# A small early write to the output, and the last store pieces issued from another queue

## The chip, the cores and the metric

The kernel runs on one core of a Trainium2 chip. The metric is the device time of one execution in microseconds (us). The time before is 471.92 us (median of 4 runs, 471.72 to 472.5; the prediction had only the first three, with a median of 471.87). The span in the profile is about 1.8 us shorter than the time, because it begins with the first recorded work. One core can show no difference between two dies, so the profiled runs with several timings are called fast by their closeness to each other; a run with a single timing has the state unknown, and of those only the trace is read here, never a time difference of a few tenths. Each trace is of one execution.

## The reference

```python
def setup_inputs():
    batch, seq, dim = (32, 512, 2048)
    return {'x': np.random.randn(batch, seq, dim).astype(np.float32)}

def reference(x):
    half_dim = x.shape[-1] // 2
    x1, x2 = (x[..., :half_dim].copy(), x[..., half_dim:].copy())
    silu_x1 = x1 * (1 / (1 + np.exp(-x1)))
    return (silu_x1 * x2).astype(np.float32)
```

So 134.2 MB are read, 67.1 MB are written, and each element gets one activation and one multiply.

## The kernel before

The profile names the engines ACT (ScalarE), DVE (VectorE), SP (SyncE, which only issues transfers here) and POOL. What SP issues and what ACT issues go through two DMA queues, and both queues are served by the same 16 DMA engines; a packet is what a DMA engine moves in one go, 64 KB of a load or 32 KB of a store here.

There are 16 tiles of 128 partitions by 8 rows. A load brings 8.4 MB and is issued from SP; a store takes 4.2 MB away and is issued from ACT. ScalarE and VectorE work on a tile in four pieces of two rows. Only the last tile is also stored in four pieces.

```python
K = 8; KC = 2
in_pool  = ctx.enter_context(tc.tile_pool(name="in_pool", bufs=2))
out_pool = ctx.enter_context(tc.tile_pool(name="out_pool", bufs=2))
xv = x_flat.rearrange("(n p k) d -> n p k d", p=P, k=K)
ov = out_flat.rearrange("(n p k) d -> n p k d", p=P, k=K)
# ... load(i): nc.sync.dma_start(out=xt, in_=xv[i])
load(0)
load(1)
for i in range(n_tiles):
    xt = loaded.pop(i)
    last = i == n_tiles - 1
    ot = out_pool.tile([P, K, half], dt, name="ot")
    for c in range(0, K, KC):
        ce = c + KC
        nc.scalar.activation(out=ot[:, c:ce, :], in_=xt[:, c:ce, :half], func=Silu)  # (name cut)
        nc.vector.tensor_mul(out=ot[:, c:ce, :], in0=ot[:, c:ce, :], in1=xt[:, c:ce, half:])
        if last:
            nc.scalar.dma_start(out=ov[i][:, c:ce, :], in_=ot[:, c:ce, :])
    if not last:
        nc.scalar.dma_start(out=ov[i], in_=ot)
    if i + 2 < n_tiles:
        load(i + 2)
```

Of the kernel before, what the change touches and what calls it, by code (L numbers as in the profile page):

```python
# [1 line left out]

# [4 lines left out]


@with_exitstack
def kernel(  # L10
    ctx: ExitStack,
    tc: tile.TileContext,
    x: bass.AP,
    out: bass.AP,
):





    nc = tc.nc
    P = nc.NUM_PARTITIONS

    x_flat = x.flatten_outer_dims()
    out_flat = out.flatten_outer_dims()
    num_rows, in_cols = x_flat.shape
    half = in_cols // 2
    dt = x_flat.dtype

    K = 8  # L30
    KC = 2
    n_tiles = num_rows // (P * K)
    assert n_tiles * P * K == num_rows

    in_pool = ctx.enter_context(tc.tile_pool(name="in_pool", bufs=2))
    out_pool = ctx.enter_context(tc.tile_pool(name="out_pool", bufs=2))

    xv = x_flat.rearrange("(n p k) d -> n p k d", p=P, k=K)
    ov = out_flat.rearrange("(n p k) d -> n p k d", p=P, k=K)

    loaded = {}

    def load(i):
        xt = in_pool.tile([P, K, in_cols], dt, name="xt")
        nc.sync.dma_start(out=xt, in_=xv[i])  # L45
        loaded[i] = xt
# [9 lines that stand above are left out]
            nc.scalar.activation(  # L56
                out=ot[:, c:ce, :],
                in_=xt[:, c:ce, :half],
                func=mybir.ActivationFunctionType.Silu,
            )  # L60
            nc.vector.tensor_mul(  # L61
                out=ot[:, c:ce, :],
                in0=ot[:, c:ce, :],
                in1=xt[:, c:ce, half:],
            )
            if last:
                nc.scalar.dma_start(out=ov[i][:, c:ce, :], in_=ot[:, c:ce, :])  # L67
        if not last:
            nc.scalar.dma_start(out=ov[i], in_=ot)
        if i + 2 < n_tiles:  # L70
            load(i + 2)


# [1 line left out]
_INS = ['x']  # L75
_OUTS = [((32, 512, 1024), 'float32')]


# [23 lines left out]
```

## Time and profile before

| What | Value |
|---|---|
| time | 471.92 us |
| span of the profiled run | 470.1 us |
| bytes moved by DMA | 201.35 MB, 428 GB/s over the span |
| VectorE, ScalarE busy | 30%, 25% |
| first store issued | 33.62 us |
| last load landed | 451.97 us |
| last store piece issued | 465.37 us |

From the page of the kernel before: the span, the busy time of two engines, the DMA row (one digit for each of 40 slices, 9 is 90% busy or more), and the issues with their size and the time from issue to landing.

```profile
span 470.1 us, 267 instructions
DVE 142.4 (30%) x64; ACT 118.3 (25%) x65; POOL 0.2 (0%) x4
DMA  8999999999999999999999999999999999999998
...
out_dram<-ot ACTq DMA_DIRECT2D x15, 4096.0 KB, 39.7
out_dram<-ot ACTq DMA_DIRECT2D x4, 1024.0 KB, 5.4
xt<-in_x_dram SPq DMA_DIRECT2D x16, 47.1
```

The DMA engines are the bound: they are busy in every slice, while no compute engine reaches a third. One period of the chain that ended last (start, length, what):

```profile
56.76 47.04 DMA xt<-in_x_dram
...
103.89 1.92 ACT ot L56
...
105.83 8.91 DVE ot L61 x4
...
114.75 47.19 DMA xt<-in_x_dram
```

From 56.76 to 114.75 us are 58.0 us for two tiles of 12.58 MB, so 434 GB/s. Only the two ends of the execution can give anything.

The timeline of the last tile (start, length, engine, line, operation, in brackets the idle time before it and who ended it), and below it the one entry of the waits list for ScalarE that belongs to the tail:

```profile
452.05 5.51 ACT L56 ACTIVATE ot<-xt 128x2048 f32<-128x2048 f32 x3 [21.65 <-DMA xt<-in_x_dram]
453.99 6.70 DVE L61 TENSOR_TENSOR ot<-ot,xt 128x2048 f32<-128x2048 f32 x3 [20.06 <-ACT ot L56]
456.32 4.74 ACTq L67 DMA_DIRECT2D out_dram<-ot  x3
461.11 1.91 ACT L56 ACTIVATE ot<-xt 128x2048 f32<-128x2048 f32 x1 [3.54 <-DVE ot L61]
463.05 2.29 DVE L61 TENSOR_TENSOR ot<-ot,xt 128x2048 f32<-128x2048 f32 x1 [2.36 <-ACT ot L56]
465.37 0.34 ACTq L67 DMA_DIRECT2D out_dram<-ot  x1
```

```profile
ACT ot L56 <- DVE ot L61: 3.5, 1, 3.5
```

The three issues on ACT wait for their multiplies, and the fourth activation stands behind them in ACT's program: it starts 3.54 us late, so the last piece is issued 13.4 us after the last load landed (465.37 - 451.97).

Three stretches of the windows view (window, length, busy time of DVE, ACT and POOL with counts, clock, share of the DMA engines, GB/s). This view books a packet whole at one instant, so a window in which no engine passes from one packet to the next shows 0 although the engines are at work.

```profile
37.00:39.40 2.40, 0.00 (x0) 0.00 (x0) 0.00 (x0) 1.00 0.00 0
458.00:460.00 2.00, 2.00 (x2) 0.00 (x0) 0.00 (x0) 1.00 0.97 410
465.00:466.50 1.50, 0.34 (x1) 0.00 (x0) 0.00 (x0) 1.00 0.37 153
```

An undisturbed 64 KB load packet takes 2.42 us and the engines are not all in phase. That no engine changes packets for 2.4 us after 37 us is unusual; the packet records say why. Here is one engine around the first store (queue, bytes, start, end):

```
load   65536   33.80   36.24
load   65536   36.24   39.55     <- 3.31 us instead of 2.42
store  32768   39.54   40.76
load   65536   40.75   43.17
```

All 16 engines have one such packet, and no later store has it. I call the surplus over the usual duration a *stretch*, and quote the sum over the engines divided by 16: 0.95 us here. The last window above is the idle time before the last piece.

### The profile page before, as it was taken

To read this page: it belongs to the slowest core of one execution; us is meant where nothing else is said; L and a number is where in the kernel's file an instruction comes from. 1 tells how busy PE (TensorE), PEld (TensorE's weight loads), DVE (VectorE), ACT (ScalarE), POOL (GpSimd) and SP (SyncE) were. 2 spreads that over 40 slices of the span, in tenths; PEclk is the share of its full clock that TensorE was granted. 3 is DMA by queue.
4 is the path that set the end of the run, shared out by engine and by line. 5 is a ranking of instruction groups with operands and counts; after the bars stand their busy time and mean duration, and the time that the engine had idled before them with its cause. 6 is when DMAs were issued, how large, how long until landed. Compare 5 with 4: busy or idle time off the path is not lost.

```text
span 470.1 us, 267 instructions
## 1 busy us (share of the span) xinstructions
DVE 142.4 (30%) x64; ACT 118.3 (25%) x65; POOL 0.2 (0%) x4
## 2 busy tenths in 40 slices
DVE  0070704207052070511606115070250702407033
ACT  1050506014060240602306032060320604106041
POOL 0000000000000000000000000000000000000000
DMA  8999999999999999999999999999999999999998
GB/s 357 446 446 401 401 485 435 418 401 443 449 446 401 441 457 396 446 474 390 468 404 438 457 441 407 427 420 449 446 410 432 480 401 418 440 474 424 399 424 337
DMA packets 5042, 201.35 MB, mean 428 GB/s; under 512 B 560, under 2 KB 560, under 8 KB 560
## 3 DMA queue, kind: packets, MB, share of 16 engines
q1 hardware_dynamic: 2304, 134.22, 66.2%
q10 hardware_dynamic: 2736, 67.11, 33.1%
q14 instruction: 2, 0.02, 0.0%
HBM read 134.22 MB, written 67.11 MB: 428 GB/s over the span
## 4 chain that ended last, share of the span: by engine, by line
DMA 80%; DVE 15%; ACT 4%; issue 0%; ACTq 0%; SPq 0%
DMA xt<-in_x_dram 80%; DVE ot L61 15%; ACT ot L56 4%; SPq L45 0%; ACTq L67 0%; ACTq L56 0%
## 5 line engine op out<-in xcount | busy, mean ns | idle before, releaser
L61 DVE TENSOR_TENSOR ot<-ot,xt 128x2048 f32<-128x2048 f32 x64 | 142.4, 2286 | 322.9 <-ACT ot L56 322.9
L56 ACT ACTIVATE ot<-xt 128x2048 f32<-128x2048 f32 x64 | 117.1, 1898 | 344.0 <-DMA xt<-in_x_dram 340.4
L56 ACT ACT_TABLE_LOAD x1 | 1.3, 1283 | 0.7 <-PEq L86 0.7
L86 POOL MEMSET const-bfloat16-1.0<- 128x1 bf16 x1 | 0.1, 101 | 0.0
L86 POOL MEMSET const-uint8-127<- 128x1 uint8 x1 | 0.1, 101 | 0.0
L86 POOL MEMSET const-float32-0.0<- 128x1 f32 x1 | 0.1, 98 | 0.2 <-issue 0.2
L86 POOL MEMSET const-float32-1.0<- 128x1 f32 x1 | 0.1, 98 | 0.0
## 6 DMA issues: line engine op xcount, KB each, us to landing
out_dram<-ot ACTq DMA_DIRECT2D x15, 4096.0 KB, 39.7
out_dram<-ot ACTq DMA_DIRECT2D x4, 1024.0 KB, 5.4
xt<-in_x_dram SPq DMA_DIRECT2D x16, 47.1
```

The lines of the kernel that those rows point to most:

```text
L56: nc.scalar.activation(out=ot[:, c:ce, :], in_=xt[:, c:ce, :half], func=mybir.ActivationFunctionType.Silu,)
L61: nc.vector.tensor_mul(out=ot[:, c:ce, :], in0=ot[:, c:ce, :], in1=xt[:, c:ce, half:],)
L86: nc = _bacc.Bacc("TRN2", target_bir_lowering=False, num_devices=1)
```

## The change

The intent: let each DMA engine do its first write to the output at the start, where nothing is lost, so that it does not cost 1 us at the first store; and let SP, which has nothing to do at the end, issue the last pieces, so that ScalarE's last activation is not held back.

```diff
+    first_pool = ctx.enter_context(tc.tile_pool(name="first_pool", bufs=1))
+    zt = first_pool.tile([16, 128], dt, name="zt")
+    nc.vector.memset(zt, 0.0)
+    nc.scalar.dma_start(out=ov[0][:16, 0, :128], in_=zt)
 
     loaded = {}
 # ... cut
             if last:
-                nc.scalar.dma_start(out=ov[i][:, c:ce, :], in_=ot[:, c:ce, :])
+                nc.sync.dma_start(out=ov[i][:, c:ce, :], in_=ot[:, c:ce, :])
```

The 16 rows of 512 bytes fall one on each DMA engine. The store of tile 0 overwrites them.

## The prediction

> **What bounds the kernel.** The DMA engines: the page's DMA row reads 9 in nearly every slice, 201.35 MB at 428 GB/s; VectorE is busy 30%, ScalarE 25%. The chain of waits repeats every 58.1 us for two tiles, so 25.17 MB / 58.1 us = 433 GB/s. The Trainium skill, "DMA: Bandwidth & Descriptors", section "Where 436 GB/s comes from", gives a ceiling of 435; this trace agrees, so the middle can't be shortened. By the packet records each engine moves 128 load packets of 64 KB (2.42 us), 120 store packets of 32 KB (1.21) and 32 of 8 KB (0.31): 465 us of the 470.1 us span. The other 5 us: 1.73 to the first packet, 0.7 by which the first load packet is longer, about 0.9 at the first store, 0.1 to 1.4 near the end, 1.3 after the last packet.
>
> **Part 1, the small write.** The first store is issued at 33.62 us. On all 16 engines one packet is stretched then: the load packet that begins at 36.2 to 36.9 us takes about 3.4 us instead of 2.42, so each engine loses 0.75 to 1.12 us (median about 0.97). No later store shows it. It delays all later loads and lies wholly on the critical path. The change lets each engine write 512 bytes at the start, where the first load packet is itself still waiting. It adds a VectorE memset (about 0.1 us, estimated from POOL's memsets) and an ACT issue (about 0.35 us), while both idle until 22.7 us. Store 0's wait on the small write is satisfied long before. If the stretch is a once-only cost of an engine's first write and overlaps the first load's start, up to 0.97 us is gained; if merely moved to the start, nothing; if it belongs to a queue that wakes from idle, or to the first mixing of loads and stores, it stays at 36 us. I expect 0.6 us on average.
>
> **Part 2, the last pieces from SP.** On ACT the issues of pieces 0 to 2 wait for VectorE and hold back the last activation (timeline: it starts at 461.11 us after 3.5 us of waiting for DVE). From SP, the activations run back to back, the last multiply ends near 453.99 + 4 x 2.23 = 462.9 instead of 465.34, and piece 3 is issued 2.4 us earlier. But the DMA engines have pieces 1 and 2 until 465.0 to 466.14 us; they idle only until piece 3 starts at 466.2 to 466.36: most over 1 us, the slowest 0.07 us. The slowest sets the end, so about 0.2 us is gained, up to 1 us if that engine (it lost 1.0 us near 314 us) isn't late this time. I expect 0.3 us.
>
> **Prediction.** 471.87 - 0.6 - 0.3 = 471.0 us, 8 in 10 between 470.1 and 472.0. Faster by over 2%: 0.01; within 2%: 0.98; slower: 0.01.
>
> **What would show it.** Right: no stretched packet or rate dip at 36 to 40 us; load 1 lands near 45.0 us instead of 45.87; the period stays 58.1 us; ScalarE's last four activations are contiguous; no engine idles between the last pieces. Wrong: the dip at 36 us remains (part 1 void), or the first load lands about 1 us later than 22.73 us (cost only moved), or a stretch appears at SP's first store (cost per queue).
>
> **What would make it wrong.** Mainly the stretch being tied to the queue's wake-up; else noise of some 0.4 us.

## The result

| | before | after |
|---|---|---|
| time, median | 471.92 us (4 runs) | 472.0 us (4 runs, 471.62 to 472.25) |
| span of the profiled run | 470.1 us | 470.5 us |
| stretch near 36 us, mean of 16 engines | 0.95 us | 1.07 us |
| stretch near 458 us | 0 | 0.61 us |
| idle of the engines in the tail | 0.92 us | 0.01 us |
| end of the last packet: median engine, last engine | 468.80, 468.88 us | 468.62, 469.14 us |

The ratio is 0.9999, with a 95% interval of 0.9982 to 1.0016: the same. (A ratio here is the mean time of one kernel's fast runs over that of the other's of the same rounds, so not quite the ratio of the medians quoted.) The rows three to six come from the packet records of the two profiled runs. Idle in the tail is the mean time in which an engine has no data packet, from the end of the last load packet to the first engine's end.

From the page of the kernel after:

```profile
span 470.5 us, 272 instructions
DVE 142.5 (30%) x65; ACT 118.2 (25%) x65; POOL 0.2 (0%) x4
...
out_dram<-ot SPq DMA_DIRECT2D x4, 1024.0 KB, 5.8
xt<-in_x_dram SPq DMA_DIRECT2D x16, 47.1
out_dram<-zt ACTq DMA_DIRECT2D x1, 8.0 KB, 9.7
```

The timeline of the last tile after:

```profile
452.50 7.31 ACT L64 ACTIVATE ot<-xt 128x2048 f32<-128x2048 f32 x4 [21.59 <-DMA xt<-in_x_dram]
454.44 8.90 DVE L69 TENSOR_TENSOR ot<-ot,xt 128x2048 f32<-128x2048 f32 x4 [20.00 <-ACT ot L64]
456.76 6.94 SPq L75 DMA_DIRECT2D out_dram<-ot  x4
```

The four activations are contiguous. The last multiply ends at 463.34 us, 10.9 us after the last load landed at 452.41 us, where it was 13.4 us before. This part did what it was meant to.

The same three windows after:

```profile
37.00:39.40 2.40, 0.00 (x0) 0.00 (x0) 0.00 (x0) 1.00 0.00 0
458.00:460.00 2.00, 2.00 (x2) 1.80 (x2) 0.00 (x0) 1.00 0.85 287
465.00:466.50 1.50, 0.00 (x0) 0.00 (x0) 0.00 (x0) 1.00 1.02 431
```

The window at 37 us is as it was: the early write removed nothing. The window at 465 us went from 153 to 431 GB/s: the idle time before the last piece is gone. But the window at 458 us fell from 410 to 287 GB/s: there is a new hole, where the first packet of SP's first piece takes up to 1.34 us instead of 0.31 (on 13 engines by more than 0.3 us). SP's first store also takes long to issue. These are the durations of the four issues from SP, shortest, median and longest, in ns:

```profile
L75 SPq DMA_DIRECT2D out_dram<-ot x4: 332/340/1057, 456.8 to 463.4; - x4
```

### The profile page after: what moved, and what is told of

Its sections match the earlier page's. It is cut to its first block, busy times and chain, and to the rows that moved or that the text cites. A ratio compares the mean times of both kernels' runs of the same rounds, so it can differ in the third digit from the quotient of the medians.

```text
span 470.5 us, 272 instructions
## 1 busy us (share of the span) xinstructions
DVE 142.5 (30%) x65; ACT 118.2 (25%) x65; POOL 0.2 (0%) x4
## 4 chain that ended last, share of the span: by engine, by line
DMA 80%; DVE 15%; ACT 3%; DVEq 0%; issue 0%; SPq 0%; ACTq 0%
DMA xt<-in_x_dram 80%; DVE ot L69 15%; ACT ot L64 3%; DVEq L105 0%; SPq L53 0%; ACTq L64 0%
```

## The experiments

Each run has one profile; those with 5 rounds also have times. The first questions are to which half of the change each finding belongs, and what the stretch at 36 us belongs to. Theory A: it is what a queue costs when it starts from empty beside a busy one. Theory B: it is a once-only cost of the first full-size store of a queue.

### The small write alone

The change without its second half (pieces again from `nc.scalar`).

> The small write alone, the last pieces issued from ACT as before. Theory A (a queue that wakes from idle beside a streaming queue stalls the DMA engines once, each time) and theory B (the first full-size store of a queue stalls it, once): the load packet stretched by about 1.0 us near 36 us stays, load 1 lands near 45.9 to 46.0 us, the tail is that of the kernel before (DMA engines idle about 1 us before the last piece), time within 0.3 us of before. My prediction's theory (first write of an engine, hidden at the start): stretch gone, load 1 lands near 45.0, time 0.6 to 1.0 us lower.

The time was 472.05 us against 471.98 (ratio 1.0005, 0.9993 to 1.0018). The stretch near 36 us was 0.82 us on average, on all 16 engines, and nothing was stretched near 458 us. So the small write does nothing for the first store, and the hole at 458 us is not its doing. Load 1 landed at 46.9 us rather than near 46.0, because one engine lost 1.34 us at 37 us and 0.67 us more at 42 us.

### The last pieces from SP alone

The change without the small write.

> The last pieces from SP alone, no small write. Theories A and B: the stretch at 36 us as before; near 458 us the first packet of SP's first store is longer by about 0.8 us on most engines, and the idle 1 us before the last piece is gone, so the time is within 0.4 us of before. If the small write were what costs in the tail, there would be no stretch at 458 us and the time would be 0.2 to 0.5 us lower.

The time was 471.92 us against 471.98 (1.0003, 0.9989 to 1.0016). The stretch at 458 us was 0.59 us, the idle time before the last piece 0.01 us. Both tail effects, the gain and the new loss, belong to the move to SP.

### The small write late, while the loads stream

```diff
-    nc.vector.memset(zt, 0.0)
-    nc.scalar.dma_start(out=ov[0][:16, 0, :128], in_=zt)
 # ... in the loop
+        if i == 0:
+            nc.vector.tensor_copy(out=zt, in_=xt[:16, 0, :128])
+            nc.scalar.dma_start(out=ov[0][:16, 0, :128], in_=zt)
```

> The small write is issued near 23 us instead of 1 us (it waits for a copy from tile 0), while load 1 streams alone. Theory A (wake from idle): a load packet near 25 to 28 us is stretched by about 1 us on each engine, and since the store queue is idle again by 33 us, another near 36 us. Theory B (first full-size store): nothing near 25 us, the stretch near 36 us as before.

The timeline line of the small write, and the window at 37 us:

```profile
22.82 0.38 ACTq L62 DMA_DIRECT2D out_dram<-zt  x1
```

```profile
37.00:39.40 2.40, 0.00 (x0) 0.00 (x0) 0.00 (x0) 1.00 0.00 0
```

No packet between 10 and 30 us was stretched, though the queue started from empty beside streaming loads; the stretch at 36 us stayed (0.91 us). Theory A, as a cost of any start, falls: and the stretch was not merely hidden in the start of the execution either. (A small write alone could not rule out that only large packets pay for a start. The two runs with an early packet of 32 KB, below, do: ACT's queue was empty again before the first regular store, and no packet at it was longer by more than 0.12 us.)

### One store in the middle from SP

```diff
-            nc.scalar.dma_start(out=ov[i], in_=ot)
+            eng = nc.sync if i == 7 else nc.scalar
+            eng.dma_start(out=ov[i], in_=ot)
```

with the last pieces from SP, without the small write.

> The store of tile 7 goes from SP, so that ACT's store queue runs empty before the store of tile 8 wakes it, and SP has issued a full-size store long before its tail pieces. Theory A: no stretch when SP issues store 7 (its queue is busy with loads), about 1 us per engine when ACT issues store 8 (near 295 us), and again about 0.8 us near 458 us. Theory B: a stretch at store 7 only, none at store 8, none at 458 us. A third, that SP's first store is merely slow to issue (1.06 us after the change, 0.34 for the others): 0.34 us issue and no stretch at 458 us here.

Store 7 was the first full-size store of SP's queue, and nothing was stretched at it. ACT's queue had run empty, and when store 8 (issued at 256.91 us, not near 295 us as I had written) woke it, the packets were 0.12 to 0.29 us longer, not 1 us. The first kills theory B in its form "per queue"; the second shows that a restart of the queue later costs far less. The stretch at 36 us belongs to the execution's first full-size store, then, not to each queue's.

In the tail SP's issues were no longer slow:

```profile
L67 SPq DMA_DIRECT2D out_dram<-ot x4: 332/338/344, 457.5 to 464.1; - x4
L70 SPq DMA_DIRECT2D out_dram<-ot x1: 348/348/348, 230.5 to 230.5; - x1
```

14 engines had no stretch there, but they did not win: the loads landed later (the last tile's work starts at 453.28 us, not at 452.05), the store queue was drained by 458.0 to 458.4 us, and most of those engines simply stood idle for 0.1 to 0.6 us. The two engines that were still busy when SP's piece came (until 458.62 and 458.86 us) were stretched by 0.8 and 0.9 us.

### All stores from SP

```diff
-            nc.scalar.dma_start(out=ov[i], in_=ot)
+            nc.sync.dma_start(out=ov[i], in_=ot)
```

and the last pieces from SP as well.

> Every store goes from SP, in the queue of the loads; ACT's queue is never used. If the stretch of 1 us at the first store belongs to the first full-size store of an execution, whatever its queue: a packet longer by about 1 us stands at the change from load 1 to store 0 (near 41 us). If it belongs to the second queue's start: no stretched packet after the first load's. In the tail SP's stores are warm, so issues of 0.34 us and no gap between pieces. Time: without the stretch 470.2 to 470.8 us, with it 471.0 to 471.6 us; if one queue cannot overlap loads and stores as well as two do, slower than before by several us.

The time was 475.69 us against 471.9 (1.0084, 1.007 to 1.0098): clear of the noise. The first two lines are windows of this run: one at its first store, one over the middle; the line in the second fence is the same middle window of the kernel before.

```profile
39.20:42.00 2.80, 0.00 (x0) 0.00 (x0) 0.00 (x0) 1.00 0.00 0
60.00:440.00 380.00, 115.66 (x52) 95.02 (x52) 0.00 (x0) 1.00 1.00 432
```

```profile
60.00:440.00 380.00, 115.67 (x52) 95.02 (x52) 0.00 (x0) 1.00 1.00 434
```

The stretch came at the change from load 1 to store 0, 1.20 us on average, in a queue that had been busy since the start. So it does not need a second queue. The loss comes on top: in one queue, the load packet before a store is on some engines 0.2 to 0.5 us longer, at nearly every tile (1.22 us per engine in the middle, 0.06 before), unevenly, so that the last engine ended at 471.48 us and the median one at 468.58. Whether this is the same effect in a weaker form is not shown; if it is, the stretch is once-only in two queues alone. Two queues are worth keeping for this kernel.

### What size must the early write have?

Three kernels with another early write from ACT, and the last pieces from ACT. First one packet of 32 KB on each engine (16 rows of 32 KB, from an output buffer):

```diff
+    zt = out_pool.tile([P, K, half], dt, name="ot")
+    nc.vector.memset(zt[:16], 0.0)
+    nc.scalar.dma_start(out=ov[0][:16], in_=zt[:16])
```

> The early write is one packet of 32 KB on each engine, the size of a store packet, instead of 512 bytes; it is issued some us after the start because its memset is longer. If the stretch belongs to the first full-size store packet: a stretched packet of about 1 us near 10 to 15 us and none at 36 us, so the time is about 1.2 us above before (the 512 KB written twice) or the same plus 1.2. If it belongs to many packets (a full store with 8 per engine) or to the first load-and-store mix of the kernel proper: stays near 36 us.

Then eight packets of 4 KB on each engine, the same bytes:

```diff
+    zt = first_pool.tile([128, 1024], dt, name="zt")
+    nc.vector.memset(zt, 0.0)
+    nc.scalar.dma_start(out=ov[0][:, 0, :], in_=zt)
```

> The early write is 8 descriptors of 4 KB on each engine (128 rows), issued near 2 us. Same question as with one packet of 32 KB, by count instead of packet size. If the count or the bytes matter: no stretch at 36 us (it is at the start or hidden there). If only the packet size matters: the stretch stays at 36 us, about 1.0 us.

Then eight packets of 512 bytes on each engine:

```diff
+    zt = first_pool.tile([128, 128], dt, name="zt")
+    nc.vector.memset(zt, 0.0)
+    nc.scalar.dma_start(out=ov[0][:, 0, :128], in_=zt)
```

> The early write is 8 descriptors of 512 bytes on each engine (128 rows by 128 columns): the count of a full store at the size of the small write, 64 KB in all. If the count matters: no stretch at 36 us and the time lower by 0.5 to 1 us. If bytes or packet size matter: the stretch of about 1.0 us stays at 36 us.

Windows at the first regular store: the first fence is the run with one packet of 32 KB, the second that with eight of 4 KB. That store is issued at 36.07 us in the first and at 34.77 us in the second, not at 33.62 us, so the windows lie later.

```profile
38.40:40.80 2.40, 0.00 (x0) 0.00 (x0) 0.00 (x0) 1.00 0.98 423
```

```profile
38.20:40.60 2.40, 0.00 (x0) 0.00 (x0) 0.00 (x0) 1.00 0.00 0
```

Only the one packet of 32 KB took the stretch away: no packet between 30 and 45 us was stretched. With eight packets of 4 KB it was 0.88 us, with eight of 512 bytes 1.09 us. Bytes and count are therefore not what matters, the size of a packet is. The 32 KB packet did not come free: 1.35 us of stretch per engine stood between 12 and 18 us, on the load packets and on the early packet itself. The early write was also extra traffic of 0.5 MB (1.2 us by the duration of a 32 KB packet), and both big writes had a span of 471.7 us, above the 470.1 of before.

### The same large packet from another buffer

The run before took its packet from an output buffer, the small writes from a buffer of their own. To part that from size, one packet of 32 KB on each engine was stored out of the first load's buffer:

```diff
+        if i == 0:
+            nc.scalar.dma_start(
+                out=ov[i][:16].rearrange("p (k two) d -> p k (two d)", two=2),
+                in_=xt[:16, :4, :],
+            )
```

(Its values are overwritten by store 0, which is issued at 35.16 us; the last of these packets ended at 30.94 us.)

> One packet of 32 KB on each engine is stored near 23 us from the buffer of load 0 instead of an output buffer, while load 1 streams alone; no memset. Theory D (the stretch is a once-only cost of the first large store packet of an execution): about 1 us of stretch near 25 to 29 us, none at the first regular store (near 37 us). If the output buffers, and not the packet size, had made the difference in the run with one early 32 KB packet: no stretch near 27 us, about 1 us at the first regular store.

Windows of this run, at the early packet and at the first regular store:

```profile
27.10:29.80 2.70, 2.70 (x2) 2.70 (x3) 0.00 (x0) 1.00 0.00 0
37.00:39.40 2.40, 0.00 (x0) 0.00 (x0) 0.00 (x0) 1.00 1.01 437
```

The packet records decide it, as the engines are less in phase here: again no stretch on the first regular store, and only 0.4 us on two engines near 30.5 us, so the buffer is not what matters. The early packet lost 2.53 us per engine, more than the 1 us expected, and the one time was 476.37 us. Its source is 16 neighbouring partitions. The Trainium skill, "SBUF — State Buffer", section "Door 1: The DMA port swizzle", says which of 16 ports a partition is reached through; by its formula partitions 0 to 15 share four ports. An estimate from that page and the 1.21 us of an ordinary 32 KB packet is 4 x 1.21 = 4.8 us for such a packet; here they took 3.07 to 4.00 us, in the run before 1.65 to 2.84 us. That could explain a part or all of the surplus in both runs, but no run separates it from the once-only cost, and the run with packets of 8 KB, below, does not bear it out. So the runs show that a large packet earlier takes the stretch away from the first store; what the once-only cost is by itself at the earlier place they do not show.

### Is SP's first store slow because it is the first?

In the changed kernel SP's first store took 1.06 us to issue. Here the small write goes from SP, between loads 0 and 1, so that SP has issued a store before the tail:

```diff
-    nc.scalar.dma_start(out=ov[0][:16, 0, :128], in_=zt)
     load(0)
+    nc.sync.dma_start(out=ov[0][:16, 0, :128], in_=zt)
     load(1)
```

> As the changed kernel, but the 512-byte write goes from SP, between loads 0 and 1, so that SP has issued a store before the tail. Theory that SP's first store of an execution is slow to issue: the first tail issue takes 0.34 us, not 0.76 to 1.06; the stretch near 458 us is gone or under 0.3 us on nearly all engines; no idle before the last piece either; time 0.2 to 0.8 us below before. The stretch at 36 us stays. Rival (the load queue must wake from idle in the tail): first tail issue and stretch near 458 us as after the change, time as before.

The time was 471.96 us against 471.85 (0.9999, 0.9986 to 1.0013). The issues in the tail:

```profile
L75 SPq DMA_DIRECT2D out_dram<-ot x4: 332/338/515, 456.5 to 463.2; - x4
```

The longest issue halved, to 0.52 us; the stretch near 458 us stayed at 0.57 us. The slow issue is thus not the cause of the hole, or not alone. What remains is the rival, that SP's queue starts anew there.

The same with 8 KB in one packet on each engine:

```diff
-    zt = first_pool.tile([16, 128], dt, name="zt")
+    zt = first_pool.tile([16, 2, half], dt, name="zt")
-    nc.sync.dma_start(out=ov[0][:16, 0, :128], in_=zt)
+    nc.sync.dma_start(out=ov[0][:16, 0:2, :], in_=zt)
```

> As the run with the write from SP, but of 8 KB in one packet on each engine (0.3 us of DMA time). If a packet of 8 KB is large enough for theory D: no stretch at 36 us, a stretch near 22 us after load 0 instead (the cost moved), time as with the 512-byte write from SP plus 0.3 us. If not: the stretch at 36 us stays, and the limit lies between 8 and 32 KB.

The time was 472.27 us against 471.85 (1.0011, 0.9999 to 1.0024). The stretch at 36 us was 1.13 us: 8 KB in a packet is not enough. The source was 16 neighbouring partitions here too, as with the packet of 32 KB, so those partitions alone do not explain what the large packet did. Nor did they slow the packets: all 16 took the ordinary 0.31 us, where the estimate above would give 4 x 0.31 = 1.24 us. The limit lies between 8 and 32 KB, if it is no matter that these 8 KB went through SP's queue and the 32 KB through ACT's; no run tests that. The stretch at 458 us was 0.54 us.

### The tail without a new queue

The last test gives the tail all that the move to SP wanted, on the queue that is running: only piece 0 is issued before the last activation, pieces 1 to 3 behind it.

```diff
-            if last:
-                nc.scalar.dma_start(out=ov[i][:, c:ce, :], in_=ot[:, c:ce, :])
+            if last and c >= 2 * KC:
+                for s in (range(0, KC, KC) if c == 2 * KC else range(KC, K, KC)):
+                    nc.scalar.dma_start(out=ov[i][:, s : s + KC, :], in_=ot[:, s : s + KC, :])
```

> No small write; the last pieces stay on ACT, but only piece 0 is issued before the last activation, pieces 1 to 3 behind it, so no activation waits for VectorE and the store queue never runs empty. If the changed kernel's tail gain was eaten by SP's queue starting anew: no stretched packet near 458 us, no idle of about 1 us before the last piece, the last multiply ends about 2.4 us earlier than before, and the span is 0.3 to 1.0 us shorter (time 471.0 to 471.6 us). If the end is set by something else (slowest engine, completion): within 0.2 us of before. The stretch at 36 us stays as it is.

The time was 472.01 us against 472.01 (0.9996, 0.9982 to 1.001). The timeline of its last tile, and two windows:

```profile
452.35 5.51 ACT L56 ACTIVATE ot<-xt 128x2048 f32<-128x2048 f32 x3 [21.59 <-DMA xt<-in_x_dram]
454.29 8.90 DVE L61 TENSOR_TENSOR ot<-ot,xt 128x2048 f32<-128x2048 f32 x4 [20.01 <-ACT ot L56]
456.61 0.34 ACTq L69 DMA_DIRECT2D out_dram<-ot  x1
457.76 1.89 ACT L56 ACTIVATE ot<-xt 128x2048 f32<-128x2048 f32 x1
458.81 4.74 ACTq L69 DMA_DIRECT2D out_dram<-ot  x3
```

```profile
458.00:460.00 2.00, 2.00 (x2) 1.65 (x1) 0.00 (x0) 1.00 0.93 389
465.00:466.50 1.50, 0.00 (x0) 0.00 (x0) 0.00 (x0) 1.00 0.96 404
```

Both holes are gone: no packet near 458 us is stretched and the engines are idle for 0.01 us. The stretch at 458 us therefore went with the move to SP's queue, which had run empty; with all stores from SP, where that queue was still busy, no packet near 458 us was stretched either, so it is not SP as such. Why this start costs 0.6 us, and ACT's later restarts between nothing and 0.29 us, is open. And yet the time is the same. The ends of the last packets on the engines (first, median and last engine) show where the gain is:

```
before                                   468.73   468.80   468.88
after                                    468.08   468.62   469.14
pieces from SP alone                     467.85   468.45   469.00
small write from SP, pieces from SP      467.88   468.63   468.94
pieces on ACT in another order           467.47   467.73   468.99
```

The median engine ends 1.07 us earlier than before in the last kernel, and the last engine does not. In the kernel before, all engines wait for the last piece to be issued, so they end together. When that wait is taken away, each engine ends when it has moved its bytes, and two engines are late (468.78 and 468.99 us; the other 14 end by 468.05). In this run the latest one had lost 1.2 us in its first packet against 0.7 us on most, and 0.3 + 0.56 us near 311 us; it finished piece 2 at 466.5 us, where most finished it at 465.0 to 465.6, and 2.45 us later it was done. Such a loss near 292 to 315 us, of 0.8 to 1.0 us on one engine and mostly less on another, stands in the trace of nearly every run.

The traces also show what it comes with. The page of each run lists a third queue, "instruction"; its packet records hold two packets of 8 KB within the span. Here is the latest engine of this run:

```
store         32768   309.57   310.78
instruction    8192   310.78   311.09
load          65536   311.08   314.06     <- 2.98 us instead of 2.42
```

In all 14 traces the two losses stand where these two packets do: each takes 0.31 us, and the packet behind it is 0.23 to 0.59 us longer. With all stores from SP both come at 370.0 us, and the losses with them. The row of that queue in short windows of the DMA view: the kernel before from 313 to 314.5 us, this run from 310 to 312 us, all stores from SP from 368 to 372 us.

```profile
q14 instruction: 2, 0.02, 2.6%
q14 instruction: 2, 0.02, 1.9%
q14 instruction: 2, 0.02, 1.0%
```

An estimate from this: without the 0.87 us the latest engine would have ended at 468.1 us, and the other late engine, at 468.78 us, would have set the end, only 0.1 us before the 468.88 us of the kernel before. No kernel beats the kernel before.

## Why the prediction was right or wrong

The time fell inside the range, but on its upper edge, and "within 2%" was right, which for a change of 1 us in 470 was not hard. The 0.9 us that I expected did not come, from neither part; that the time still fell inside is owed to the width of the range and not to the mechanism.

- **The bound** was read correctly. The middle runs at 434 GB/s before and after, and nothing moved there. The Trainium skill's 435 GB/s ("DMA: Bandwidth & Descriptors", "Where 436 GB/s comes from") agrees with it; the lower limit of about 358 GB/s, which the same section gives for transfers between HBM and SBUF, is not what this one core shows.
- **Part 1, expected 0.6 us, measured nothing** (stretch 0.95 us before, 1.07 after). The step that failed is "a once-only cost of an engine's first write", met by the 512-byte write. It is once-only, and tied to the first full-size store, as the run with one store from SP and the run with all stores from SP show. But a first write is not enough: packets of 512 bytes (one or eight), of 4 KB (eight) and of 8 KB (one) left it, one of 32 KB took it away. The alternatives that I named were near but not it: a queue's wake-up was ruled out by the late small write, and the mixing of loads and stores needs to be said with the packet's size. What happens in the engine in that microsecond is not shown by any run.
- **Part 2, expected 0.3 us, measured nothing.** The mechanism up to the issue was right: activations contiguous, the last multiply 2.4 us earlier after the last load, no idle before the last piece. Two things took it back. One I had named only as a sign of error, a stretch at SP's first store: it was 0.6 us on average, came with the start of SP's queue beside the draining store queue, and the tail in another order on ACT has none. The other was in the prediction as "the slowest sets the end", with a gain of 0.2 us left over; the last experiment shows that this is all there is: even with no hole at all, the last engine ended at 468.99 us against 468.88. The prediction left up to 1 us open in case the engine that had lost 1.0 us near 314 us was not late this time; but two instruction packets delay some engine in every execution that was profiled.
- **The costs of the addition** were right: the memset took 0.17 us, the ACT issue 0.43 us, both while those engines were idle, and the small write's packets took 0.03 us each.

## What to carry to other kernels

A warm-up must resemble what it is to warm: here only a packet of the store's own size took the once-only cost away, and it cost more than it saved (spans of 471.7 and 474.6 us against 470.1). Work is not gained by issuing it earlier from another queue without looking at whether that queue is running. And when a tail is made tighter, read the end of the last packet on each DMA engine: the kernel ends with the latest engine, and a microsecond won on fourteen of them is worth nothing.

## What the Trainium skill lacked or had wrong

- "DMA: Bandwidth & Descriptors" does not tell of the once-only cost at an execution's first large store: one packet on each engine is, on average, 0.8 to 1.2 us longer at it in every kernel whose earlier writes were at most 8 KB a packet (0.95 us on average in the kernel before), and none where a packet of 32 KB had gone before.
- The same page, "Issuing engines are not separate DMA queues", says that the issuing engine only saves the sequencer's time. Here loads and stores through one queue instead of two cost 0.84% (475.69 against 471.9 us), and moving the last pieces to a queue that had run empty stretched their first packets by 0.6 us on average.
- The same page has a row on engines that are usually slower, which it ties, as a guess, to transfers issued from GpSimd; it gives nothing on how differently the 16 engines of one core end with transfers from SP and ACT. With no idle time left, first and last ended 1.5 us apart (467.47 and 468.99 us).
- The same page names refill among a core's internal queues, but no page gives what the packets of the "instruction" queue take from a stream of data: two packets of 8 KB, 0.31 us each, with the packet behind each 0.23 to 0.59 us longer (near 292 to 315 us in 13 traces, at 370 us with all stores from SP).
